# A two-layer attention and retention trunk: tokens' norm-weight products on GpSimd, norms and rotation tables in numbered rounds, and a first rotation read from PSUM

## The chip, the core and the metric

The kernel runs on one core of one Trainium2 chip. The metric is the device time of one execution in microseconds (us). The engines are named as in the profile: PE is TensorE, PEld its weight loads, DVE is VectorE, ACT is ScalarE, POOL is GpSimd, and SP is SyncE, whose queue issues all DMAs of this kernel. Each engine works through its own instructions in order.

## The reference

The input is a sequence of 2048 tokens of width 1024. Two layers follow one another, and then a last RMS norm. One layer, with `h = RMSNorm(x) * gain`:

```python
proj = h @ w_in                       # 1024 x 4096: aq ak av ag rq rk rv rg, 512 columns each
ya = chunked_rel_attention(aq, ak, av, rel_bias)    # 8 heads x 64, own chunk of 64 and 8 before it
yr = chunkwise_retention(rq, rk, rv, cos, sin)      # 4 heads x 128, q and k rotated, state with decay
y  = concat[ya * silu(ag), yr * silu(rg)]
x  = x + y @ w_out                    # 1024 x 1024
```

The rotation takes the two halves of a head's 128 columns, `t1` and `t2`, to `t1*cos - t2*sin` and `t1*sin + t2*cos`. The angles are the positions times 64 fixed frequencies. All is float32, and the kernel gives every large product in float16 parts: a value is split into an upper half (its float16) and a lower half (the float16 of what remains), and three products (upper-upper, upper-lower, lower-upper) are summed.

## The kernel before, in words

**Tiles and stages.** Tokens lie in 16 tiles of 128, four tiles make a block of 512 (`n` = 0 to 3). A layer's columns are worked in four sections (`s` = 0 to 3): a section has two attention heads and one retention head. For each `(l, s, n)` the kernel runs `dense_T` (L608), which makes the four feature-major products q, k, rotated q and rotated k (`j` = 0 to 3; 24 matmuls of 512 columns each, L731), then `dense_V` (L738), which makes the token-major products of four token tiles (`a` = 0 to 3; values and gates, 24 matmuls each, L752). The attention and retention of block `n` run beside the dense products of block `n + 1`. After the four sections of a layer, `wout` multiplies by `w_out`.

**Rounds.** `dense_T` and `dense_V` are generators that yield after every eight matmuls of 512 columns. `run` (L1176) takes one such step, then `tick` (L598), which executes what was put off with `later(k, ...)` for k rounds, then one step of the attention (a unit takes three rounds: scores, maximum, exponential, split, transpose), and then steps of the background work list `bg` (`push`, `pull`). How many steps it pulls follows from the steps left and the rounds left. I call such a turn a round. Round 0 is the first of `dense_V(0, 0, 0)`. Block 1 has rounds 12 to 23 (`dense_T`) and 24 to 35 (`dense_V`), block 2 has 36 to 59, block 3 has 60 to 83, and section 1 begins with round 84. The text numbers rounds for both kernels in this way; the kernel before does not count them.

**The order of the engines** is the program's order for PE, ACT, DVE and POOL. SP's order is the program's only up to the end of `dense_V(0, 0, 0)` (`sp_order`, L1245 and L1446); after that the framework's planner places the DMAs.

**Start.** The first block's work is written out by hand in a list of steps (L1387 to L1390), of which `d` is a step of the first `dense_T`, `t` of the first rotation table, `xsq4` the squares of token tile 4, and so on. The steps for tiles 4 to 7 go on in a list of twelve rounds (L1392) beside `dense_V(0, 0, 0)`; a `u` in it is a step of the second table, a `bt` one of the bias tiles.

**A token tile's norm.** Tile `t` of `x` is loaded, ACT sums its squares (`sq`), DVE and POOL make the reciprocal root (`root`, a power on POOL, L212), DVE multiplies the tile by the root and the norm's gain (`mul`, L254 or L1207), ACT writes the upper half (`hi`), DVE the lower half (`lo`, L276 or L231), and two DMA transposes bring both into `hT` (`dma`, L236 and L237). Tiles 8 to 15 go through `norms_from_input` (L1190), pushed as background work of 21 steps in blocks 1 and 2, each step together with a step of the next rotation table (`tables`, L83).

**Tables.** `tables(n)` loads 512 positions, makes the angles in two halves of 256 columns, reduces them by multiples of 2 pi on DVE, takes two sines on ACT (L121, L122), negates one on DVE (L124), and writes cosine and sine to DRAM with eight DMAs (L129 to L132). `tab_load` (L613) reads them back for a block.

**Rotation.** In `dense_T`, for `j` = 2 and 3, `evacuate` copies the product from PSUM by ACT (L662). `swap` exchanges the halves of its partitions with two DMAs (L666, L667). Three DVE operations turn it (L686 to L688), and an upper and a lower half follow. For the first block, this begins in round 4 for `j` = 2 and ends in round 14 for `j` = 3. `decayed` (L870) multiplies the rotated k by the rotated q of one token tile; its first call stands in the attention, in round 14.

**Preparation of section 1.** `prep_T` (25 steps) and `prep_V` (23 steps) load and split the next section's weights. PE sums the column squares over partitions with a product with ones (`allsum`, L319), three steps after ACT squared them; `lowp` (L314) casts the sums to bfloat16 before. They are pushed at the start of block 3 and of its `dense_V`.

## Time and profile before

| | us |
|---|---|
| median of 3 runs | 2083.68 (2080.86 to 2083.72) |
| the profiled execution, device time | 2085.9 |
| its span, first to last instruction | 2084.1 |
| PE busy | 2005.3 (96%) |
| DVE busy | 1345.9 (65%) |
| ACT busy | 1141.0 (55%) |
| POOL busy | 435.8 (21%) |
| mean granted PE clock | 0.991 of full speed |

The profile is of one execution. Busy times are shares of the span; an engine's busy time does not say what it waited for, so the stretches with waits are looked up in the timelines of the engines. A row of a timeline gives the start, the duration, the engine, the source line, the operation, the written and read tiles, the shape, and in brackets the idle time ahead of it with what ended it.

### The profile page before, as it was taken

How to read it: one execution, taken by the hardware profiler on the slowest of the kernel's cores; microseconds unless marked ns; L12 is line 12 of the kernel's file. 1: busy time of each engine (PE TensorE's matmuls, PEld its weight loads, DVE VectorE, ACT ScalarE, POOL GpSimd, SP SyncE). 2: the span in 40 equal slices, each digit the busy share in tenths (PEclk: the TensorE clock that was granted, in tenths of full speed). 3: DMA queues.
4: the chain of work that ended last, by engine and by line, in shares of the span. 5: the costliest groups of instructions: out<-in, count | busy, mean ns of one | idle time of the engine just before them, and what ended most of it. 6: DMA issues, size and time to landing. Idle time of an engine off the chain costs nothing. (4 is left out here: it accounts for less than half of the span.)

```text
span 2084.1 us, 39559 instructions
## 1 busy us (share of the span) xinstructions
PE 2005.3 (96%) x14014; PEld 1051.2 (50%) x14014; DVE 1345.9 (65%) x4031; ACT 1141.0 (55%) x2522; POOL 435.8 (21%) x509
## 2 busy tenths in 40 slices
PE   6888999999999999999999999999999999999998
PEld 4334454555555555544444555555555555555443
DVE  7677666666666666676654667666666666667643
ACT  7455565556565654565444546554655665446432
POOL 1022221222122222231000222222222222222100
PEclk9999999999999999999999999999999999999999
DMA  8767775557567764699875556655755766557874
GB/s 250 169 121 164 142 158 113 120 102 158 121 147 147 158 158 99 134 221 256 219 187 118 121 102 138 134 120 102 149 125 125 174 153 166 121 117 176 212 199 124
DMA packets 645702, 313.65 MB, mean 150 GB/s; under 512 B 459232, under 2 KB 602080, under 8 KB 645504
## 3 DMA queue, kind: packets, MB, share of 16 engines
q1 hardware_dynamic: 645504, 311.12, 66.3%
q8 instruction: 110, 1.80, 0.4%
q14 instruction: 88, 0.72, 0.1%
HBM read 123.26 MB, written 41.98 MB: 79 GB/s over the span
## 5 line engine op out<-in xcount | busy, mean ns | idle before, releaser
L810 POOL TENSOR_TENSOR pq<-sc,pq 128x640 f16<-128x640 f32 (+4 forms) x256 | 324.7, 1269 | 1165.6 <-issue 625.4
L807 ACT ACTIVATE sc<-sc,mq,cT 128x640 f32<-128x640 f32 (+4 forms) x256 | 218.5, 853 | 552.0 <-DVE mq L806 416.9
L731 PE MATMUL dT<-hTh,whT 128*128 128x512 f16 x1008 | 351.5, 385 | 15.8 <-DMA hTh<-hTl 9.7
L752 PE MATMUL dV<-whV,hTh 128*128 128x512 f16 x1024 | 352.9, 380 | 10.0 <-DVE gt L770 9.9
L752 PE MATMUL dV<-whV,hTl 128*128 128x512 f16 x1024 | 353.0, 380 | 0.0
L752 PE MATMUL dV<-wlV,hTh 128*128 128x512 f16 x1024 | 352.7, 380 | 0.0
L731 PE MATMUL dT<-hTh,wlT 128*128 128x512 f16 x1008 | 346.6, 379 | 0.0
L731 PE MATMUL dT<-hTl,whT 128*128 128x512 f16 x1008 | 346.6, 379 | 0.0
L752 PEld LDWEIGHTS <-hTh 128*128 128x128 f16 x2048 | 196.6, 98 | 223.1 <-DVE gt L770 13.7
L731 PEld LDWEIGHTS <-whT 128*128 128x128 f16 x2016 | 193.2, 98 | 223.8 <-issue 26.9
L804 DVE CUSTOM_DVE_ANT_0 sc<-S,bias 128x640 f32<-128x640 f32 (+4 forms) x256 | 188.6, 737 | 70.5 <-PE S L801 64.5
L809 ACT ACTIVATE pq<-sc 128x640 f16<-128x640 f32 (+4 forms) x256 | 171.5, 670 | 10.5 <-DMA pT<-pq 2.5
L1129 PE MATMUL dO<-whO,yly 128*128 128x512 f16 x448 | 170.3, 380 | 2.2 <-DMA yly<-rly 1.5
L1129 PE MATMUL dO<-whO,yhy 128*128 128x512 f16 x448 | 170.3, 380 | 0.4 <-DMA yhy<-hTh 0.4
L1129 PE MATMUL dO<-wlO,yhy 128*128 128x512 f16 x448 | 170.2, 380 | 0.0
L752 PEld LDWEIGHTS <-hTl 128*128 128x128 f16 x1024 | 99.5, 98 | 104.0 <-issue 1.4
L731 PEld LDWEIGHTS <-wlT 128*128 128x128 f16 x1008 | 97.3, 98 | 101.8 <-issue 1.1
L800 PE MATMUL S<-k,q 128*128 128x128 f16 (+3 forms) x592 | 143.3, 268 | 1.9 <-DVE mq L804 1.8
L1129 PEld LDWEIGHTS <-yhy 128*128 128x128 f16 x896 | 87.5, 98 | 101.9 <-issue 1.1
L820 PE MATMUL o<-v,pT 128*128 128x65 f16 x1120 | 130.4, 194 | 8.1 <-DMA pT<-pq 7.6
L821 PE MATMUL o<-v,pT 128*128 128x64 f16 x1120 | 130.6, 195 | 0.0
L801 PE MATMUL S<-k,q 128*128 128x128 f16 (+3 forms) x592 | 130.4, 268 | 0.0
(361 smaller groups left out, 3412.0 us busy)
## 6 DMA issues: line engine op xcount, KB each, us to landing
q<-qq SPq DMA_DIRECT2D x128, 128.0 KB, 2.6
yyy<-y_d SPq DMA_DIRECT2D x32, 512.0 KB, 4.7
stT<-in_w_in_dram SPq DMA_DIRECT2D x27, 512.0 KB, 4.6
stV<-in_w_in_dram SPq DMA_DIRECT2D x26, 512.0 KB, 4.6
k<-kk SPq DMA_DIRECT2D x128, 64.0 KB, 2.0
swp<-rot SPq DMA_DIRECT2D x64, 128.0 KB, 2.5
tabc<-tab SPq DMA_DIRECT2D x32, 256.0 KB, 2.7
tabs<-tab SPq DMA_DIRECT2D x32, 256.0 KB, 2.9
```

Source lines behind the costliest of these rows:

```text
L731: pe.matmul(ps, w_[:, j, kt, :], h_[:, kt, :], start=(m == 0), stop=(m == 23))
L752: pe.matmul(ps, h_[:, kt, a * P:(a + 1) * P], w_[:, kt, :], start=(m == 0), stop=(m == 23))
L800: pe.matmul(o, st.q[:, hx, 0, cs], k_, start=True, stop=False)
L801: pe.matmul(o, st.q[:, hx, 1, cs], k_, start=False, stop=True)
L804: dve.tensor_tensor_reduce(out=v, in0=S[:, 0:w], in1=g.bias[hx][:, 640 - w:640], scale=1.0, scalar=-3.0e38, op0=ALU.add, op1=ALU.max, accu ...
L807: act.activation(v, v, AF.Exp, bias=m[:, 0:1], scale=g.c[:, 0:1])
L809: act.activation(pq[:, 0:w], v, AF.Copy)
L810: pool.tensor_tensor(pq[:, w:2 * w], v, pq[:, 0:w], op=ALU.subtract)
L820: pe.matmul(o[:, 0:65], u.p[:, b, :], v_[:, 0:65], start=(b == 0), stop=False)
L821: pe.matmul(o[:, 0:64], u.p[:, b, :], v_[:, 65:129], start=False, stop=False)
L1129: pe.matmul(ps, h_[:, kt, :], w_[:, kt, :], start=(m == 0), stop=(m == 23))
```

## The change

What it does, part by part:

- **Products with the norm's gain.** For token tiles 4 to 15 POOL multiplies the tile by the gain, without the root; the root enters as the scale of the ACT copy (upper half) and of the DVE operation (lower half).
- **Numbered rounds.** `run` counts rounds, and `slot(r, fn)` puts work into round r. Tiles 8 to 11 begin their squares in rounds 18, 21, 24, 27, tiles 12 to 15 in rounds 39, 42, 45, 48; each is loaded four rounds earlier, its upper half comes three, its lower half four and its transposes five rounds later. The second table ends in rounds 12 and 14, the third has rounds 18 to 38 and the fourth 36 to 56. The preparation of section 1 is pulled 48 times in rounds 57 to 95. In the list beside `dense_V(0, 0, 0)` the second table's steps rise from ten to fourteen.
- **Cut products.** In block 1, section 0, the products `j` = 0 and 1 are made by token tiles (128 columns), tile 7 last.
- **First rotation.** For the first block, DVE reads the product from PSUM: a cosine product, two half sine products that write to the other half of the partitions, and a sum; there is no copy by ACT and no swap. Both j fall into rounds 3 to 9, the transposes of k into round 11, and the first `decayed` into round 10.
- **Tables.** The negation of a sine is ACT's, directly after the sines, and the cosine is written by one DMA for two copies: six DMAs for eight.
- **Casts of sums.** Where two sums are added and then cast, one DVE operation does both.

The diff, cut to its core:

```diff
@@ tables
         act.activation(r, ang, AF.Sin)
         act.activation(k2, k, AF.Sin)
-        yield
-        dve.tensor_scalar(ang, r, -1.0, None, op0=ALU.mult)
-        yield
+        act.activation(ang, r, AF.Copy, scale=-1.0)
+        yield
+        d = tab_d[n].rearrange("i (b p) (a c) -> i b a p c", b=2, a=2)
         for hf in range(2):
             sl = slice(hf * 64, hf * 64 + 64)
-            cs = slice(hf * 256, hf * 256 + 256)
-            sp.dma_start(tab_d[n][0, 0:64, cs], k2[sl, :])
-            sp.dma_start(tab_d[n][0, 64:128, cs], k2[sl, :])
-            sp.dma_start(tab_d[n][1, 0:64, cs], ang[sl, :])
-            sp.dma_start(tab_d[n][1, 64:128, cs], r[sl, :])
+            sp.dma_start(d[0, :, hf].rearrange("b p c -> p b c"), k2[sl, None, :].to_broadcast([64, 2, 256]))
+            for b, t_ in enumerate((ang, r)):
+                sp.dma_start(d[1, b, hf], t_[sl, :])
@@ Tok
         def mul(self):
+            if self.rows:
+                pool.tensor_tensor(self.x, self.x, gains[0].b, op=ALU.mult)
+                return
...
-                act.activation(self.rw[0], self.x, AF.Copy)
+                rows_hi(self.rw, self.x, self.r)
...
-                dve.tensor_tensor(self.rw[1], self.x, self.rw[0], op=ALU.subtract)
+                rows_lo(self.rw, self.x, self.r)
@@ sums and casts
-        if len(sts) == 2:
-            dve.tensor_tensor(m1[:, 0:1], m1[:, 0:1], m1[:, 1:2], op=ALU.add)
-        return m1[:, 0:1]
+        return [m1[:, i:i + 1] for i in range(len(sts))]
...
+        if more is None:
+            dve.tensor_copy(mb, m1)
+        else:
+            dve.tensor_tensor(mb, m1, more, op=ALU.add)
@@ dense_T
+        def first_rotation(j, ps, rot):
+            if j == 2:
+                st.rq = rot
+                later(1, tab_load)
+                own = rot[:, 1:3].rearrange("p a c -> p (a c)").bitcast(F32)
+            else:
+                st.rk = rot
+                own = b1.tile([P, 512], F32, tag="qq", name=f"raw{nm}")
...
+            def cosine():
+                dve.scalar_tensor_tensor(out=own, in0=ps, scalar=2.0 ** -16, in1=st.tabc, op0=ALU.mult, op1=ALU.mult)
+
+            def sine(half):
...
+                dve.scalar_tensor_tensor(out=st.swp[o_], in0=ps[i_], scalar=-2.0 ** -16, in1=st.tabs[i_], op0=ALU.mult,
+                                         op1=ALU.mult)
...
+            d = 2 * j
+            later(d, cosine)
+            later(d, lambda: sine(0))
+            later(d + 1, lambda: sine(1))
+            later(d + 2, lambda: dve.tensor_tensor(own, own, st.swp, op=ALU.add))
+            later(d + 3, lambda: act.activation(rot[:, 0], own, AF.Copy))
+            later(d + 4, lambda: dve.tensor_tensor(rot[:, 1], own, rot[:, 0], op=ALU.subtract))
+            if j == 2:
+                later(d + 5, lambda: act.activation(rot[:, 2], rot[:, 0], AF.Copy, scale=2.0 ** -11))
+            else:
+                later(d + 6, tokens)
...
+        parts = (l, s, n) == (0, 0, 1)
+        if parts:
+            ps, m = [None] * 2, 0
+            for (j, a) in ((0, 0), (0, 1), (0, 2), (1, 0), (1, 1), (1, 2), (0, 3), (1, 3)):
...
+                    pe.matmul(ps[j][:, cs], w_[:, j, i % KT, :], h_[:, i % KT, cs], start=(i == 0), stop=(i == 23))
+                    m += 1
+                    if m % 32 == 0 and m < 192:
+                        yield
+                if a == 3:
+                    evacuate(j, ps[j])
+            yield
@@ attention
-            elif a == 0 and (l, s, n) == (0, 0, 0):
-                decayed(l, s, n, g, st, 0)
@@ run
+            for fn in slots.pop(ring["round"], ()):
+                fn()
+            ring["round"] += 1
+            if left is None:
+                continue
@@ norms_from_input
+            def mul():
+                pool.tensor_tensor(u.x, u.x, gains[0].b, op=ALU.mult)
+
+            for i, fn in ((-4, load), (0, sq), (0, mul), (1, root), (3, lambda: rows_hi(rows, u.x, u.rs)),
+                          (4, lambda: rows_lo(rows, u.x, u.rs)), (5, lambda: transpose_rows(rows, *u.h))):
+                slot(r + i, fn)
@@ steps and rounds
-       "Vhi2 Vhi3 d d Vlo2 Vlo3 xsq5 d Vu d xsq6 xrs4 d Vu xmul4 xsq7 d")
+       "Vhi2 Vhi3 d d Vlo2 Vlo3 xsq5 xmul4 d Vu d xsq6 xrs4 xmul5 d Vu xsq7 xmul6 d")
-    push(rounds(["xhi4 xrs5 xrs6", "xlo4 xmul5 xrs7", "xdma4 xhi5 xmul6 bt", "xlo5 xhi6 u", "xdma5 xlo6 xmul7", "xdma6 xhi7",
-                 "xlo7", "xdma7 u", "u u bt", "u u bt", "u u", "u u bt"]), 12)
+    push(rounds(["xhi4 xrs5", "xlo4 xrs6 xmul7", "xdma4 xhi5 xrs7 bt", "xlo5 u", "xdma5 xhi6 u", "xlo6 u", "xdma6 xhi7 u",
+                 "xlo7 u u", "xdma7 u u bt", "u u bt", "u u", "u u bt"]), 12)
+    table_steps(t1, (12, 12, 14))
+    table_steps(t2, [18] + list(range(22, 36)) + [36, 38])
+    table_steps(t3, [36] + list(range(40, 54)) + [54, 56])
+    norms_from_input(18, range(8, 12), late[0:4])
+    norms_from_input(39, range(12, 16), xs0[0:2])
+    first_prep = 57
+    for r in range(first_prep, 96):
+        for _ in range((r + 1 - first_prep) * 48 // 39 - (r - first_prep) * 48 // 39):
+            slot(r, lambda: pull(1))
+    slot(first_prep - 1, lambda: push(prep_T(0, 1, grp(0, 1)), 25))
...
-                if (n, s) == (0, 0) and not first:
+                if (n, s) == (0, 0):
                     later(11, lambda n=n, g=g, st=st: decayed(l, s, n, g, st, 0))
```

129 lines of the change are left out of this document (61 added, 68 removed).

## The prediction

> **What bounds the kernel now.** I read the page's first part, then the waits of TensorE, then busy time by windows cut at the points where TensorE changes its token block, then the engines' timelines around each hole. TensorE is the bound:
>
> ```profile
> PE 2005.3 (96%) x14014; PEld 1051.2 (50%) x14014; DVE 1345.9 (65%) x4031; ACT 1141.0 (55%) x2522; POOL 435.8 (21%) x509
> 360.00:2084.10 1724.10, 1699.36 (x11882) 886.82 (x11879) 1098.92 (x3279) 929.38 (x2068) 367.96 (x412) 1.00 0.66 148
> 47.70:78.50 30.80, 21.10 (x97) 9.21 (x96) 18.71 (x38) 14.61 (x31) 1.90 (x5) 0.89 0.84 188
> 78.50:140.40 61.90, 51.95 (x293) 25.18 (x294) 46.35 (x135) 35.22 (x75) 10.88 (x18) 0.94 0.60 129
> 140.40:206.60 66.20, 57.47 (x398) 29.98 (x398) 46.54 (x127) 36.14 (x75) 15.50 (x18) 0.91 0.73 150
> 206.60:260.00 53.40, 48.51 (x352) 25.65 (x353) 33.21 (x113) 31.12 (x68) 11.98 (x11) 0.95 0.71 144
> 260.00:360.00 100.00, 95.41 (x703) 50.65 (x701) 65.10 (x235) 59.98 (x145) 22.39 (x30) 1.00 0.63 136
> ```
>
> In a window's row the first number is its length, the second TensorE's busy time, and the number after POOL's the granted clock. From 360 us on TensorE is idle for 1724.1 - 1699.4 = 24.7 us of 1724, and there the change only swaps tiny casts. Between 47.7 and 360 us the idle time is 9.7 + 9.9 + 8.7 + 4.9 + 4.6 = 37.9 us, at a clock of 0.89 to 0.95 up to 260 us. This is the whole of the first weight section and the preparation of the second, and it is where the change works. What is saved in it moves all later TensorE work earlier, one for one. The two longest entries of TensorE's waits in the same stretch (line waited for: total, times, longest):
>
> ```profile
> PE dT L731 <- DMA hTh<-hTl: 9.7, 1, 9.7
> PE dV L752 <- DVE gt L770: 8.7, 4, 4.9
> ```
>
> The holes and what follows them, from TensorE's timeline (start, duration, count, idle before):
>
> ```profile
> 31.02 0.61 PE L712 MATMUL dT<-hTh,whT 128*128 128x128 f16 x8
> 32.35 0.61 PE L712 MATMUL dT<-hTh,whT 128*128 128x128 f16 x8
> ...
> 63.47 0.39 PE L752 MATMUL dV<-whV,hTh 128*128 128x512 f16 x1
> ...
> 68.45 0.38 PE L752 MATMUL dV<-wlV,hTh 128*128 128x512 f16 x1
> 78.52 3.57 PE L731 MATMUL dT<-hTh,whT 128*128 128x512 f16 x8 [9.69 <-DMA hTh<-hTl]
> ...
> 129.53 0.39 PE L752 MATMUL dV<-whV,hTh 128*128 128x512 f16 x1 [4.88 <-DVE gt L770]
> ...
> 140.36 3.47 PE L731 MATMUL dT<-hTh,whT 128*128 128x512 f16 x8 [2.44 <-issue]
> ...
> 146.31 1.89 PE L731 MATMUL dT<-hTl,whT 128*128 128x512 f16 x8
> ...
> 182.67 0.22 PE L860 MATMUL r<-sh,rot 128*128 128x128 f16 x1 [1.90 <-DVE sh L868]
> 194.32 0.39 PE L752 MATMUL dV<-whV,hTh 128*128 128x512 f16 x1 [2.68 <-DVE gt L770]
> 206.64 3.57 PE L731 MATMUL dT<-hTh,whT 128*128 128x512 f16 x8 [3.65 <-DMA hTh<-rhn]
> ```
>
> Between 63.47 and 68.45 lie 23 starts, 0.217 us each: a tile's 24 matmuls take 5.2 us and a round, a third of them, 1.73. Eight as one row show 1.89 us in a running stream and 3.47 to 3.57 right after a hole: each hole costs 1.6 us more at a lowered clock. The clock in the windows falls where the holes are. I count six such tails (after 78.5, 129.5, 140.4, 182.7, 194.3 and 206.6 us). That is 9.6 us, and with 33.3 us of idle before 260 us the stake is 43 us. By the Trainium skill, "TensorE: Matmul & The Clock Gate", section "HAM oscillation — how this bites in real kernels", only idle gaps over about 3.4 us are to be avoided; the trace differs, since the hole of 2.4 us before 140.36 has its tail too, and the measurement decides. By the page three tails fewer, 4.8 us, would be at stake.
>
> **Entry of the second token block.** Its first matmul, 78.52, waits for the transposes of token tile 7, although tile 4's products could have run. The change cuts the first two sections' products into token tiles (192 matmuls of 128 columns), tile 7 last. Three groups of eight take 32.35 - 31.02 = 1.33 us, and eight times that is 10.6 us, against two times 5.2 us, so the cut itself costs 0.2 us. The wait for tile 7 goes. What is late next? I follow VectorE, which is in order and runs behind:
>
> ```profile
> 55.47 0.29 DVE L766 SCALAR_TENSOR_TENSOR v<-dV,v 128x128 f16<-128x128 f32 x1 [1.53 <-ACT rv L762]
> 55.68 0.34 DVE L768 SCALAR_TENSOR_TENSOR rv<-dV,urvV,rv 128x128 f16<-128x128 f32 x1
> 55.94 0.41 DVE L770 SCALAR_TENSOR_TENSOR gt<-gt,dV 128x256 f32<-128x256 f32 x1
> 57.46 1.22 DVE L276 TENSOR_TENSOR hTh<-hTh,hTh 128x1024 f16<-128x1024 f32 x1
> 59.00 0.69 DVE L670 TENSOR_TENSOR rot<-rot,tabc 128x512 f32<-128x512 f32 x1 [0.32 <-DMA tabc<-tab]
> ...
> 66.63 0.29 DVE L99 CAST xa<-xa 128x256 f32<-128x256 int32 x1 [1.48 <-DMA xa<-in_pos_dram]
> 66.96 0.35 DVE L100 TENSOR_SCALAR xa<-xa,invf_sb 128x256 f32<-128x256 f32 x1
> 68.61 0.29 DVE L96 TENSOR_SCALAR xa<-xa 128x256 f32<-128x256 f32 x1
> ```
>
> In the changed kernel the first rotation is turned out of PSUM: per section cosine, two half sines and a sum, four operations on 512 columns where there were three, and both sections now fall into rounds 3 to 9 of the first value products; before, the second was turned only in rounds 10 to 14. The operations have 512 columns whatever their partitions, so I give each 0.69 us (59.00). The first decayed product stands in round 10, and it needs the second section's lower half, VectorE's last operation of round 9. Between the gate of tile 0 (55.94, ends 56.3) and that, VectorE has ten operations of 0.69 = 6.9 us, three lower halves of tokens at 1.28 = 3.8 us (1.22 at 57.46; with the scale in them I take 180.00's form, below), two sets of evacuations at 1.04 (55.47 to 55.94) = 2.1 us, and steps 2 to 8 of the second table, some ten operations of 0.29 to 0.43, 3.7 us. That is 16.5 us, less some 0.08 us of overlap between neighbours, 2 us: the half is ready near 71 us, and if the second step waits for its positions as at 66.63, near 72.5. TensorE reaches the product after two thirds of tile 3: 63.47 + 3.46 = 66.9 us. It waits 4 to 5.5 us, where before it ran through to 68.8; one tail of 1.6 follows. I take 4.5 us. A further 1 us is put down for the third section's start: in the cut order section 0's bank is freed just one tile (1.3 us) before it is wanted again, and the copy by ScalarE and the difference by VectorE (0.69 by 59.00) fit into that only if neither engine is behind. So in this window 9.7 + 1.6 goes and 4.5 + 1.6 + 0.2 + 1 comes: **4 us gained**. Its ends are 9.5 (VectorE not behind) and 0 (behind by 4 us more). On SP, four swaps and two writes of each table less are cover for the transposes; I give them nothing, since VectorE comes later.
>
> **Second block's value products, third block's entry.** The hole of 4.9 us before 129.53 waits for VectorE's gate, which waits for ScalarE:
>
> ```profile
> 124.35 1.28 ACT L121 ACT_TABLE_LOAD   x1
> 125.65 0.42 ACT L121 ACTIVATE xb<-xb 128x256 f32<-128x256 f32 x1
> 125.97 0.40 ACT L122 ACTIVATE xb<-xb 128x256 f32<-128x256 f32 x1
> 126.54 1.28 ACT L761 ACT_TABLE_LOAD   x1
> ```
>
> Two table loads and the two sines of a rotation table stand in front of the evacuation. In the changed kernel the sines come in round 12 (second table), 36 (third) and 54 (fourth). 12 and 36 open a feature-major product, whose next evacuation is three rounds (5.2 us) off and covers the 1.28 + 0.42 + 0.40 + 0.42 (the negation, new on ScalarE) + 1.28 = 3.8 us. Round 54 is within a value product, but one third into a tile, the bank wanted six rounds later. The hole of 2.4 us before 140.36 is tile 11's transposes, which come one to two rounds (1.7 to 3.5 us) earlier, in round 32 of 36. VectorE loses four products of 1.28 us in this block. Of 9.95 + 1.6 us in this window I leave 3 us (waits on scores and gates, whose causes stay): **8.5 gained**.
>
> **Third block.** Idle 8.73 us and three tails, 13.5 us: the state's half (1.9), gates, and tile 15's transposes (3.6 before 206.64). Two chains make it:
>
> ```profile
> 180.00 1.28 DVE L1207 SCALAR_TENSOR_TENSOR xin<-xin,rsn,gb 128x1024 f32<-128x1024 f32 x1 [2.55 <-POOL rsn L212]
> 188.00 1.38 DVE L827 TENSOR_TENSOR rl<-rl,kaV 128x1 f32<-128x1 f32 x1
> 179.41 0.55 POOL L212 TENSOR_TENSOR rsn<-ssn,mhalf 128x1 f32<-128x1 f32 x1
> 187.97 1.40 POOL L810 TENSOR_TENSOR pq<-sc,pq 128x640 f16<-128x640 f32 x1 [4.54 <-ACT pq L809]
> L810 POOL TENSOR_TENSOR pq<-sc,pq 128x640 f16<-128x640 f32 x192 | 271.7, 1415 | 861.0 <-issue 469.1 <-ACT pq L809 374.0 <-DMA y_d<-ya 11.2
> L1058 POOL TENSOR_TENSOR hTl<-hTl,fg 128x512 f32<-128x512 f32 x1 | 1.3, 1262 | 3.9 <-ACT fj L1054 3.9
> L827 DVE TENSOR_TENSOR rl<-rl,kaV x256: 159/159/1376, 99.0 to 1959.9; 128x1 f32<-128x1 f32 x128
> ```
>
> At 180.00 VectorE stands 2.55 us for GpSimd's root before it can multiply the token; in the changed kernel the product needs no root, is GpSimd's own, and the root enters in ScalarE's copy two rounds later. Tile 15's transposes go out in round 53 of 60 instead of about 58. I leave 5 us of the 13.5, one late start with its tail and a little more: **8.5 gained**. The cost is on GpSimd: 128x1024 by twice L1058 is 2.5 us a token, against 1.28 on VectorE. With 1.4 (L810) and two roots of 0.55 it comes to 4.5 us in a step of three rounds, 5.2 us at least; it is queued right behind the unit's difference, so it fills the gap before the next.
>
> **Preparation of the next section.** 4.9 us of idle plus a tail after 206.6: 48 steps come over 39 rounds instead of 48 over 24, so the three steps between a section's squares and TensorE's sum over them are 2.4 rounds instead of 1.5. Half goes, with the tail: **4 gained**. The casts of sums save one 128x1 operation each on VectorE, nothing on the path. After 260 us: 0.
>
> **Sum.** 4 + 8.5 + 8.5 + 4 = 25 us. The profiled execution took 2085.9 us (2084.1 of span, 1.8 around it), the median of the runs is 2083.7; the gain is the same in both: 2061 profiled, 2059 as a median.
>
> **Rivals.** *GpSimd's products hold VectorE (slower).* At 187.97 GpSimd starts a difference of 1.40 us, and VectorE's one-column product at 188.00 takes 1.38 us instead of its median 0.16. So VectorE stands for as long as GpSimd runs. Twelve products of 2.5 us could hold it 30 us, against 12 x 1.28 = 15 us of work taken off it. If TensorE pays every hold in full, 30 - 25 = 5 us slower, and with a clock tail of 1.6 at half the tokens 10 more: 2083.7 + 15 = 2099. It decides from a cost of 25 / 12 = 2.1 us a token on TensorE's path. Against it: GpSimd's differences, 192 of them of 1.4 us, run through the whole kernel already, and L827's median equals its minimum. By the Trainium skill, "SBUF — State Buffer", section "SBUF: two separate sides", the loser of the pair of ports that VectorE and GpSimd share is blocked for the whole instruction; by that rule every lower half and table step that meets a product waits it out. The trace agrees at 188.00. *The wait only moves (faster, by less).* The first decayed product takes the whole first window and each later block keeps one late start of some 4 us with its tail: 4 + 8.5 + 8.5 + 4 less 4 + 5.6 + 5.6 is 10 us, 2074. For it speaks VectorE's 46 of 62 us in the second block; against it, 5 us of products leaving there. *It doesn't start earlier.* SP, whose order after the first block is not written out, lets transposes stand behind other transfers, and rounds gained are lost there: 0 to 4 us, 2082.
>
> **Numbers.** Forecast 0.72, 2045 to 2071 (all 43 us but 4, to half of the 25); moved wait 0.13 (2071 to 2079); not earlier 0.06; held VectorE 0.09. Less than 0.2%, 4.2 us, can't be told from no change here. Faster 0.86 (forecast, moved wait, a little of the third), same 0.05, slower 0.09. The range 2045 to 2080 leaves out the slower rival, most of the third and a thin tail below.
>
> **What would show it.** Right: section products of the second block start near 72 to 75 us; TensorE waits on VectorE's half in the first decayed product, 4 to 5 us; no ScalarE table load between a value product and its evacuation in the second block; no hole over 2 us before the third and fourth block; the idle from 47.7 to 260 us falls from 33 to near 15. Wrong: VectorE rows stretched to 2 us and more beside GpSimd's products, and TensorE waiting on gates or on the transposed probabilities in rounds 18 to 50; or idle time from 360 us on that differs from 24.7 us by more than 3.

## The result and the profile after

The changed kernel is slower, by a little. Eleven runs have a median of 2089.78 us (2083.75 to 2092.8), eleven of the kernel before on the same chip 2083.68 us; the ratio on record, formed from all these runs, is 1.0022, with a 95% interval of 1.0012 to 1.0031 (the two medians alone are 6.1 us apart). Three later timings of the same program beside the kernel before gave 1.0015 (1.0007 to 1.0024), 1.0018 (1.0006 to 1.0029) and 1.0009 (0.9999 to 1.002). By these ratios the loss is 2 to 5 us, about 3.5, where 25 us of gain were forecast. The profiled execution took 2090.2 us.

The first row is from the page of the changed kernel, the others from its busy time by windows, cut where TensorE enters the second, third and fourth block, section 1's feature-major products, its value products, and at 360 us (columns as in the windows of before):

```profile
PE 2005.6 (96%) x14158; PEld 1056.5 (51%) x14158; DVE 1346.3 (64%) x4004; ACT 1141.7 (55%) x2524; POOL 465.5 (22%) x521
47.80:77.60 29.80, 23.17 (x101) 9.85 (x100) 24.35 (x49) 15.25 (x33) 10.65 (x12) 0.91 0.72 143
77.60:137.30 59.70, 52.04 (x435) 31.52 (x434) 43.05 (x114) 32.61 (x72) 20.70 (x19) 0.93 0.57 124
137.30:203.30 66.00, 55.09 (x402) 28.61 (x400) 46.97 (x119) 38.98 (x80) 26.24 (x21) 0.97 0.81 171
203.30:258.60 55.30, 52.87 (x410) 28.51 (x411) 39.25 (x134) 35.69 (x79) 13.92 (x13) 1.00 0.75 163
258.60:293.60 35.00, 28.25 (x206) 14.57 (x204) 18.40 (x68) 23.01 (x51) 8.47 (x10) 0.95 0.61 136
293.60:360.00 66.40, 65.16 (x451) 34.24 (x451) 43.27 (x160) 35.84 (x88) 12.77 (x18) 0.97 0.55 121
360.00:2088.40 1728.40, 1697.47 (x11871) 885.47 (x11868) 1092.49 (x3260) 927.45 (x2065) 365.89 (x411) 1.00 0.67 148
```

TensorE is idle for 6.6, 7.7, 10.9 and 2.4 us in the first four windows, 27.6 in all, where the kernel before had 33 up to 260 us and the forecast 15. The new hole is in the fifth window: 35.0 us for twelve rounds, with 6.8 idle and a clock of 0.95. The kernel before needs 27.7 there (a window of its own trace):

```profile
267.00:294.70 27.70, 26.36 (x204) 14.06 (x202) 15.42 (x60) 19.41 (x46) 6.99 (x8) 1.00 0.77 168
```

The holes of the changed kernel, from TensorE's timeline:

```profile
65.29 0.39 PE L808 MATMUL dV<-whV,hTh 128*128 128x512 f16 x1 [1.75 <-DVE gt L826]
70.06 0.29 PE L914 MATMUL r<-rot,rot 128*128 128x128 f16 x2 [1.14 <-ACT rot L659]
74.08 0.29 PE L914 MATMUL r<-rot,rot 128*128 128x128 f16 x1 [3.74 <-DVE rot L660]
...
117.19 0.22 PE L914 MATMUL r<-sh,rot 128*128 128x128 f16 x1 [2.24 <-DVE sh L922]
...
127.83 0.61 PE L808 MATMUL dV<-whV,hTh 128*128 128x512 f16 x1 [3.61 <-DVE gt L826]
...
177.07 0.27 PE L856 MATMUL S<-k,q 128*128 128x256 f16 x1 [3.86 <-DVE mq L860]
...
184.61 0.22 PE L914 MATMUL r<-sh,rot 128*128 128x128 f16 x1 [1.31 <-DVE sh L922]
...
193.75 0.39 PE L808 MATMUL dV<-whV,hTh 128*128 128x512 f16 x1 [1.81 <-DVE gt L826]
...
203.26 1.04 PE L787 MATMUL dT<-hTh,whT 128*128 128x512 f16 x4 [2.47 <-DVE gt L826]
...
283.93 0.16 PE L328 MATMUL msV<-mbV,ones 128*128 128x1 bf16 x1 [3.00 <-DVE mbV L318]
...
293.59 2.63 PE L808 MATMUL dV<-whV,hTh 128*128 128x512 f16 x7 [3.70 <-ACT whV L335]
```

The hole of 9.7 us before the second block is gone. In its place stand 1.75, 1.14 and 3.74 us within the first value products; in the second and third block nearly every wait is for VectorE (state's halves, gates, the maximum `mq`); and 3.00 and 3.70 us wait for section 1's value weights.

One profile of each kernel is not enough for differences of some us, so both were profiled again, unaltered. The table gives the start in us of the first matmul of each stretch, for three profiles of before and four of after; the last column is the time from the third section's first matmul to the end of the span.

| | 2nd block | 3rd block | 4th block | section 1 | its values | 3rd section | from there to the end |
|---|---|---|---|---|---|---|---|
| before | 78.5, 78.4, 76.7 | 140.4, 140.6, 139.0 | 206.6, 205.3, 203.5 | 266.9, 264.7, 261.3 | 294.7, 292.5, 289.1 | 476.8, 473.4, 470.0 | 1607.3, 1610.9, 1606.8 |
| after | 77.6, 78.1, 78.2, 78.7 | 137.3, 137.8, 137.7, 138.2 | 203.3, 205.4, 205.4, 205.8 | 258.6, 260.7, 260.6, 261.6 | 293.6, 295.7, 295.7, 296.6 | 475.1, 477.9, 477.1, 479.0 | 1613.4, 1611.5, 1611.1, 1605.3 |
| difference of means | +0.3 | -2.3 | -0.2 | -4.0 | +3.3 | +3.8 | +2.0, within the scatter |

The result is in the middle columns: 4.0 us are gained by section 1's start, 7.2 are lost in its first products (35.0 us in all four profiles, 27.7 to 27.8 in the three of before), and 3.3 remain, about the loss that the timings show.

### The profile page after: what moved, and what is told of

Read it like the earlier page. It is cut to its first block, busy times and chain, and to the rows that moved or that the text cites. A ratio compares the mean times of both kernels' runs of the same rounds, so it can differ in the third digit from the quotient of the medians.

```text
span 2088.4 us, 39808 instructions
## 1 busy us (share of the span) xinstructions
PE 2005.6 (96%) x14158; PEld 1056.5 (51%) x14158; DVE 1346.3 (64%) x4004; ACT 1141.7 (55%) x2524; POOL 465.5 (22%) x521
## 4 chain that ended last, share of the span: by engine, by line
PE 44%; DVE 3%; DMA 3%; ACT 3%; issue 2%; SPq 1%; POOL 0%; POOLq 0%; DVEq 0%; ACTq 0%
PE dT L787 14%; PE dV L808 12%; PE dO L1183 12%; PE r L914 2%; PE S L857 1%; PE S L856 1%; DMA pT<-pq 1%; DMA swp<-rot 1%; PE o L876 1%; PE o L877 1%; PE o L878 1%; ACT sc L863 1%; DVE sc L860 1%; ACT pq L865 0%; DMA x_d<-hTl 0%
## 5 line engine op out<-in xcount | busy, mean ns | idle before, releaser
L787 PE MATMUL dT<-hTh,whT 128*128 128x512 f16 x992 | 342.4, 380 | 2.5 <-DVE gt L826 2.5
L787 PE MATMUL dT<-hTl,whT 128*128 128x512 f16 x992 | 342.4, 380 | 0.0
L787 PE MATMUL dT<-hTh,wlT 128*128 128x512 f16 x992 | 342.2, 379 | 0.0
L860 DVE CUSTOM_DVE_ANT_0 sc<-S,bias 128x640 f32<-128x640 f32 (+4 forms) x256 | 188.3, 735 | 77.9 <-PE S L857 66.1
L856 PE MATMUL S<-k,q 128*128 128x128 f16 (+3 forms) x592 | 142.4, 267 | 5.0 <-DVE mq L860 5.0
L876 PE MATMUL o<-v,pT 128*128 128x65 f16 x1120 | 129.7, 193 | 16.8 <-DMA pT<-pq 16.5
L876 PEld LDWEIGHTS <-pT 128*128 128x128 f16 x1120 | 105.4, 97 | 54.9 <-DMA pT<-pq 26.2
```

The costliest lines, as they stand in the source:

```text
L787: pe.matmul(ps, w_[:, j, kt, :], h_[:, kt, :], start=(m == 0), stop=(m == 23))
L856: pe.matmul(o, st.q[:, hx, 0, cs], k_, start=True, stop=False)
L860: dve.tensor_tensor_reduce(out=v, in0=S[:, 0:w], in1=g.bias[hx][:, 640 - w:640], scale=1.0, scalar=-3.0e38, op0=ALU.add, op1=ALU.max, accu ...
L876: pe.matmul(o[:, 0:65], u.p[:, b, :], v_[:, 0:65], start=(b == 0), stop=False)
```

## The experiments

Each kernel was timed beside the kernel before on the same chip, and each ratio is to that; medians of different rows can come from different chips. In the expectations, "second section" is section 1, and the stretch "from about 476 us" (464 in the faster kernels) begins with the third section.

| kernel | median us | ratio to before (95%) |
|---|---|---|
| changed, again (e1, e15, e16) | 2087.40, 2086.60, 2085.86 | 1.0015, 1.0018, 1.0009 |
| value weights earlier (e2) | 2082.24 | 0.9989 (0.9979 to 0.9999) |
| products on VectorE (e3) | 2090.69 | 1.0026 (1.0016 to 1.0036) |
| both (e4) | 2085.94 | 1.0005 (0.9996 to 1.0014) |
| weights earlier, no products (e5) | 2072.90 | 0.9946 (0.9932 to 0.9960) |
| weights earlier, decayed product later (e6, e10) | 2075.61, 2075.10 | 0.9958 (0.9944 to 0.9972), 0.9959 (0.9943 to 0.9975) |
| changed, decayed product later (e12) | 2080.93 | 0.9991 (0.9982 to 0.9999) |
| as e6, uncut (e17) | 2075.17 | 0.9961 (0.9948 to 0.9975) |
| as e6, sines later (e18) | 2074.63 | 0.9961 (0.9949 to 0.9974) |
| before, again (e13, e14) | 2083.41, 2081.62 | 0.9994 (0.9986 to 1.0003), 0.9992 (0.9982 to 1.0003) |

### The preparation of section 1

```diff
-    for r in range(first_prep, 96):
-        for _ in range((r + 1 - first_prep) * 48 // 39 - (r - first_prep) * 48 // 39):
-            slot(r, lambda: pull(1))
+    for r0, r1, k in ((first_prep, 72, 25), (72, 90, 23)):
+        for r in range(r0, r1):
+            for _ in range((r + 1 - r0) * k // (r1 - r0) - (r - r0) * k // (r1 - r0)):
+                slot(r, lambda: pull(1))
```

> Only the pace of the second section's weight preparation is altered: the 25 steps of the feature weights in rounds 57 to 71, the 23 of the value weights in rounds 72 to 89, where the changed kernel spreads 48 evenly and ends in round 95, the last before the second section's value products. Theory (what the first section saves is given back because the value weights come by rounds): the wait of 3.0 us for the sum over the squares at 283.9 and of 3.7 us for the last converted weights at 293.6 go, the value products start 6 to 7 us sooner, near 287 us, and the time falls by about as much, 2083 to 2084. Rival (the preparation only fills VectorE and ScalarE, which are behind anyway; packing it into fewer rounds makes gates late in the fourth block): the fourth block grows by 3 to 5 us and the total stays within 2 us of the changed kernel.

Measured: section 1's first products take 28.0 us instead of 35.0, and the time is 5.2 us below that of the changed kernel beside it (2082.24 and 2087.40). The theory holds for the two waits. But the first half of the rival holds too: the fourth block takes 59.3 us where the changed kernel has 55.3, since TensorE waits again for the sums over the squares, four times, 1.1 to 1.6 us. Fourth block and first products together fall from 90.3 to 87.3 us, by 3 and not by 7 (from 90.8 in the twelfth run to 86.0 in the sixth and tenth, below). What makes the rest of the 5.2 us is open: the fourth block begins 3.5 us sooner in this profile than in that of the changed kernel beside it, before the packed steps can have saved anything. ScalarE's timeline shows the chain, first in the changed kernel (with VectorE's cast of the sum, and the two GpSimd operations ahead of the bias tile's scaling):

```profile
281.33 0.83 ACT L584 ACTIVATE bias<-bias,ciT 128x640 f32<-128x640 f32 x1 [1.97 <-DMA y_d<-ya]
282.55 1.04 ACT L310 ACTIVATE whV<-stV 128x1024 f16<-128x1024 f32 x1
...
290.69 1.13 ACT L335 ACTIVATE whV<-stV,sV 128x1024 f16<-128x1024 f32 x1
...
292.40 1.14 ACT L335 ACTIVATE whV<-stV,sV 128x1024 f16<-128x1024 f32 x1
...
283.71 0.16 DVE L318 TENSOR_TENSOR mbV<-m1V,m1V 128x1 bf16<-128x1 f32 x1 [5.35 <-ACT whV L310]
...
279.49 1.40 POOL L866 TENSOR_TENSOR pq<-sc,pq 128x640 f16<-128x640 f32 x1 [5.57 <-issue]
...
281.15 0.14 POOL L583 MEMSET bias<- 64x64 f32 x1
```

the same scaling in the second profile of the changed kernel:

```profile
283.41 0.83 ACT L584 ACTIVATE bias<-bias,ciT 128x640 f32<-128x640 f32 x1 [1.97 <-POOL bias L583]
```

and with the earlier preparation:

```profile
268.50 1.04 ACT L310 ACTIVATE whV<-stV 128x1024 f16<-128x1024 f32 x1
...
278.34 1.14 ACT L335 ACTIVATE whV<-stV,sV 128x1024 f16<-128x1024 f32 x1
...
286.01 0.83 ACT L584 ACTIVATE bias<-bias,ciT 128x640 f32<-128x640 f32 x1 [1.97 <-POOL bias L583]
```

In the changed kernel the square of the last value section stands in the program behind the scaling of a bias tile, and that waits until 281.33. The row names a transfer, `y_d<-ya`, but the scaling does not use that tile. What it waits for is GpSimd, which fills two corners of the bias tile behind its difference and ends at 281.29; the second profile names it, with the same 1.97 us. The square then ends at 283.6, TensorE's sum over it comes 3.00 us late, the two conversions at 290.69 and 292.40 follow, and the last of them is what the value products wait for at 293.59. With the steps packed into fewer rounds the square is at 268.5, the conversion at 278.3, and the bias tile comes after both, though its scaling waits the same 1.97 us.

### The products with the norm weights

```diff
-                pool.tensor_tensor(self.x, self.x, gains[0].b, op=ALU.mult)
+                dve.tensor_tensor(self.x, self.x, gains[0].b, op=ALU.mult)
...
-                pool.tensor_tensor(u.x, u.x, gains[0].b, op=ALU.mult)
+                dve.tensor_tensor(u.x, u.x, gains[0].b, op=ALU.mult)
```

In the fifth kernel both lines are left out instead.

> Only the engine of the twelve products of a token with the norm weights is altered: VectorE in place of GpSimd, in the same rounds, still without the root. Theory (GpSimd's products of 2.4 us each hold VectorE's two-operand work, so that they cost it 1.9 us a token beyond its own work, more than the 1.28 us they take off it): the eight stretched rows of VectorE (2.1 to 2.65 us at 95, 103, 114, 124, 161, 170, 182 us, 1.6 at 154) are gone; TensorE's waits of 2.2, 3.6, 3.9 and 1.3 us at 117, 128, 177 and 185 us shrink to half or less, and the second section's first block starts 3 to 6 us sooner, near 254 us. Rival (VectorE is simply full: 1.28 us of product there is as bad as the hold): it starts within 1.5 us of 258.6. By the theory that the second section's value products wait for weights that come by rounds, the time itself stays within 2 us of the changed kernel in either case, since the start of the value products stays bound.

> Both alterations together: value weights finished by round 89 and the products on VectorE. If both theories hold, the second section's first block starts near 254 us and its value products near 282, 11 us before the changed kernel; the time is 2078 to 2081. If only the preparation counts, it is that of the earlier preparation alone, 2083 to 2084. If neither, 2088 to 2091.

> The earlier value weights of the second run, and the twelve products of a token with the norm weights left out altogether (the norm weights then act only through the other factors, so the output is another one). It gives the whole price of the products: on GpSimd by comparison with the earlier preparation alone, on VectorE by comparison with that and the products on VectorE. Theory (the hold is paid on the path: eight rows of VectorE stretched by 1.6 to 2.4 us, TensorE's waits at 117, 128, 177 and 185 us behind them): the second section's first block starts 6 to 9 us sooner than with GpSimd's products, at 252 to 255 us, and the time falls by 4 to 8 us to 2074 to 2078. Rival (VectorE is late in these blocks with or without them, since rotations, tables and gates come in the same rounds): it starts at 259 to 261 us and the time stays within 2 us of 2082.

The hold that all three speak of, from GpSimd's and VectorE's timelines of the changed kernel, with a row of the same form beside each that meets no product:

```profile
113.98 2.40 POOL L1273 TENSOR_TENSOR xin<-xin,gb 128x1024 f32<-128x1024 f32 x1 [1.11 <-ACT hTh L203]
123.48 2.76 POOL L1273 TENSOR_TENSOR xin<-xin,gb 128x1024 f32<-128x1024 f32 x1 [1.11 <-ACT hTh L203]
103.27 2.12 DVE L883 TENSOR_TENSOR rl<-rl,kaV 128x1 f32<-128x1 f32 x1
111.17 0.16 DVE L883 TENSOR_TENSOR rl<-rl,kaV 128x1 f32<-128x1 f32 x1
114.45 2.48 DVE L718 TENSOR_TENSOR rot<-rot 128x512 f16<-128x512 f32 x1
129.41 0.69 DVE L718 TENSOR_TENSOR rot<-raw,rot 128x512 f16<-128x512 f32 x1
124.14 2.65 DVE L712 TENSOR_TENSOR raw<-raw,swp 128x512 f32<-128x512 f32 x1
118.62 0.68 DVE L712 TENSOR_TENSOR raw<-raw,tabc 128x512 f32<-128x512 f32 x1
```

VectorE's lower half at 114.45 takes 2.48 us, where the same operation takes 0.69 at 129.41; it ends 0.55 us behind GpSimd's product (116.38), about its own time. Eight rows of the second and third block are stretched so, at 95, 103, 114, 124, 154, 161, 170 and 182 us, by 15 us together.

Yet the theory of the third run fell: with the products on VectorE the holes are as long, only for other operands. The rival is right in that VectorE's own time for the products is as bad as the hold, but it is worse than it said: section 1 starts at 263.6 us, outside both forecasts (near 254, or within 1.5 of 258.6), and later than the 260.7 of the changed kernel beside it. The time is 3.3 us worse (2090.69 and 2087.40), where both had it within 2 us, and 3.7 us worse with the earlier weights (2085.94 and 2082.24), which is none of the three cases that the fourth run's expectation names. TensorE's timeline of the third run:

```profile
114.81 0.33 PE L914 MATMUL r<-rot,rot 128*128 128x128 f16 x3 [2.87 <-DVE dT L922]
...
130.12 0.61 PE L808 MATMUL dV<-whV,hTh 128*128 128x512 f16 x1 [4.95 <-DVE gt L826]
...
165.46 0.33 PE L914 MATMUL r<-rot,rot 128*128 128x128 f16 x3 [2.41 <-DVE dT L922]
...
181.12 0.37 PE L856 MATMUL S<-k,q 128*128 128x256 f16 x1 [3.53 <-DVE mq L860]
```

Without the products the time falls by 9.3 us to 2072.90, more than the 4 to 8 of the theory; section 1 starts at 255.3 us, and the third section 6.5 us sooner than with GpSimd's products, so some 3 us of the difference belong to the later stretch, where single executions scatter. TensorE's time in the second and third block, all three with the earlier weights, first on GpSimd, then on VectorE, then without, from the windows of each:

```profile
76.84:135.58 58.74, 48.67 (x435) 29.98 (x433) 42.75 (x113) 32.30 (x72) 20.70 (x19) 1.00 0.57 124
135.58:201.87 66.29, 54.99 (x399) 28.68 (x399) 46.76 (x120) 39.30 (x80) 26.26 (x21) 0.97 0.80 172
```

```profile
76.42:137.54 61.12, 50.31 (x435) 30.43 (x433) 39.23 (x117) 32.37 (x72) 10.67 (x15) 0.97 0.54 120
137.54:206.56 69.02, 55.30 (x399) 28.78 (x399) 42.95 (x124) 39.29 (x80) 16.38 (x17) 0.98 0.79 165
```

```profile
80.52:133.76 53.24, 49.13 (x435) 30.78 (x433) 35.46 (x113) 32.23 (x72) 10.11 (x15) 0.98 0.64 137
133.76:195.97 62.21, 54.82 (x399) 28.73 (x399) 39.29 (x120) 39.14 (x80) 16.16 (x17) 0.97 0.85 174
```

Eight products cost TensorE (58.7 - 53.2) + (66.3 - 62.2) = 9.6 us on GpSimd and (61.1 - 53.2) + (69.0 - 62.2) = 14.7 on VectorE, though no wait in the changed kernel's trace ends with GpSimd's product itself. Of a hold of 1.9 us, up to 1.2 show on TensorE, although VectorE is busy for only 43 of 59 and 47 of 66 us. (The second block of the run without products starts 3.7 us later, by a gate; at section 1's start 5.9 of the 9.6 us and 10.8 of the 14.7 are left, so both are upper ends.)

### The first decayed product

```diff
-                if (n, s) == (0, 0):
+                if (n, s) == (0, 0) and not first:
                     later(11, lambda n=n, g=g, st=st: decayed(l, s, n, g, st, 0))
...
             if hx == 1:
                 next(ret, None)
+            elif a == 0 and (l, s, n) == (0, 0, 0):
+                decayed(l, s, n, g, st, 0)
```

> The earlier value weights, and the first decayed product back where the kernel before had it, in the first attention unit's second round instead of round 10 of the first value products. In the changed kernel TensorE waits there 3.7 us at 74.1 for VectorE's lower half, and 1.1 us just before. Theory (that wait is VectorE's lateness at this one place, and a product asked for four rounds later finds its operand ready): both waits go, the second block starts 3.5 to 5 us sooner, at 72 to 73.5 us, and the time falls by 3 to 5 us to 2077 to 2079. Rival (VectorE is late for the next user too, the gates and scores of the second block, so the wait only moves): the second block starts sooner, but its value products start within 1.5 us of 100 us, and the time stays within 1.5 us of 2082.

> The changed kernel with only the first decayed product back in the attention unit, and the preparation as the change has it. Theory (gains in the first section are given back at the second section's value products, whose weights come by rounds): the second block starts near 72 us, 5 us sooner, and the second section's first block near 253 us, but its value products wait longer, and the time falls by no more than 3 us, to 2085 to 2088; with the earlier preparation the same step was worth 6.6 us. Rival (the two gains add): 2081 to 2083.

> The same kernel without the extra transfers, once more beside it: 2074 to 2077, and a second sample of its stretch from about 464 us to the end (1613 us in the first).

The first two run with and without the earlier weights, the third repeats the first. The second block starts at 71.5, 72.3 and 72.6 us, 5 to 7 sooner than in the changed kernel, behind one wait for a gate there (the sixth run's timeline):

```profile
71.50 0.62 PE L767 MATMUL dT<-hTh,whT 128*128 128x128 f16 x8 [1.52 <-DVE gt L826]
```

The time falls by 6.6 us with the earlier weights, where 3 to 5 were expected, and without them to a ratio of 0.9991, where the changed kernel has 1.0009 to 1.0022: by 4 to 6.5 us. So the theory of the twelfth run was wrong: the loss at the value products does not swallow what is gained ahead of it. Its products took 35.0 us again, starting from 254.2. The preparation is tied to rounds, rounds move with TensorE, and the 7.2 us are a fixed price; the gains add. The change with these two edits, the sixth and tenth run, is 0.4% faster than the kernel before.

### The cut and the sines

```diff
-        parts = (l, s, n) == (0, 0, 1)
+        parts = False
```

> Earlier value weights and the first decayed product in the attention unit, and the second block's first two sections uncut again, as in the kernel before: 24 matmuls of 512 columns each, the lower halves of the tokens last in the first section. With the cut the second block starts at 71.5 to 72.6 us, and token tile 7's two transposes land about 1.2 us before and 1.5 us after that. Theory (the earlier norms and the shorter queue on SP did away with the hole of 9.7 us, the cut does nothing here): the second block starts within 1 us of 72, the third block within 1 us of where it does with the cut (131.2 to 132.9), the time is 2074 to 2077. Rival (the cut is needed): a hole of 2 us or more at the start, and the third block starts 2 us or more later, 2077 to 2080.

The second block starts at 72.6 us and the third at 132.8, as in the tenth run with the cut (72.6 and 132.9), and the time is the same. The cut does nothing in this kernel. The issue of tile 7's last transpose ends at 72.2 us here (70.96 + 1.24) and at 77.3 in the kernel before (74.34 + 2.93), so the hole of 9.7 us went because the transposes come earlier. The changed kernel as it was, with the decayed product in round 10, was not run without the cut.

```diff
-    table_steps(t3, [36] + list(range(40, 54)) + [54, 56])
+    table_steps(t3, [36] + list(range(40, 54)) + [56, 57])
```

> The same two edits with the cut, and the third table's sines in round 56 and its writes in round 57, where the change has rounds 54 and 56. In round 54 two loads of ScalarE's function table of 1.28 us and three operations of 0.4 stand ahead of the evacuation of the third block's third tile, and TensorE waits 2.47 us at the start of the fourth block for the bank. Theory (the loads make that hole): it falls under 0.5 us, the fourth block starts 2 to 2.5 us sooner, 195 to 197.5 us, and the time falls by 2 us to 2072 to 2074. Rival (ScalarE or VectorE is late there anyway): the hole stays over 1.5 us and the time within 1 us of 2075.

The changed kernel's ScalarE, ahead of its hole of 2.47 us at 203.26:

```profile
197.29 1.28 ACT L121 ACT_TABLE_LOAD   x1
...
200.26 1.28 ACT L817 ACT_TABLE_LOAD   x1
201.56 0.47 ACT L817 ACTIVATE gt<-dV,ughV 128x256 f32<-128x256 f32 x1
201.93 0.36 ACT L818 ACTIVATE rv<-dV,urvV 128x128 f16<-128x128 f32 x1
```

(The expectation counts the tables from 0; it is the fourth.) With the sines in round 56 the hole is gone and the fourth block starts at 195.6 us, 1.8 and 3.6 sooner than in the sixth and the tenth run. But a sum for the weights waits 2.17 us a little later:

```profile
200.73 0.16 PE L328 MATMUL msT<-mbT,ones 128*128 128x1 bf16 x1 [2.17 <-DVE mbT L316]
```

Section 1 starts at 255.7 us (256.8 and 258.6), and the time of 2074.63 can't be told from 2075.1. The theory holds for the hole; the 2 us that it put on the time are not shown.

### The stretch after 475 us

> The changed kernel once more, unaltered. It separates what is in the program from what differs between executions. If the loss after 475 us is part of the program (instructions arriving 6 us earlier or later fall differently against the probability transposes), the second profile again starts the second section's first block near 258.6 us and its value products near 293.6, and again spends 4 to 6 us more than the kernel before between 475 us and the end. If it is scatter between executions, the landmarks up to 475 us agree within 0.5 us and the stretch from there to the end differs from the first profile by several us. Time by either: 2084 to 2092.

> The earlier value weights, and twelve loads' worth of extra transfers of 512 bytes each, one in each round from the third on of the second section's second block (about 322 to 345 us): as many as the change took off SP's queue. All waits on probability transposes after 475 us that the five changed kernels show and the kernel before does not (at about 491, 525, 908, 950, 1296, 1711, 1912 us) come from instructions that are the same in both. Theory (it is SP's place in its own instruction stream: its fetches of 16 KB every 17 us each hold it for about 1 us, and fall on other transfers when there are fewer instructions ahead of them): twelve more shift them back, most of these waits go, and the time falls to 2077 to 2080. Rival (the loss comes with the buffers' other places, or with the moment at which the stretch begins): the waits stay where they are, and the time is 2082 to 2083.

> The kernel before with four extra transfers of 512 bytes in the same place, rounds 3 to 6 of the second section's second block; nothing before 320 us differs. It gives the semaphores of all later transfers the places that they have in the changed kernel (eight in turn, and twelve fewer is four on), and shifts SP's instruction stream by four transfers. Theory (the later loss is a matter of SP's place in its stream or in the turn of semaphores): waits on probability transposes appear at about 491, 525, 908 and 950 us, and the time rises by 3 to 6 us to 2087 to 2090. Rival (it comes with other buffers or another starting moment): the tail is as in the kernel before, 2083 to 2085.

> Earlier value weights, first decayed product in the attention unit, and twelve extra transfers of 4 bytes kept in their places in SP's order, between about 275 and 340 us (in the run with twelve transfers they had gone ahead of the second block, and cost 17 us there). Theory (the later loss is a matter of SP's place in its instruction stream or of the turn of semaphores, which twelve transfers fewer had shifted): from the second section's last block (about 464 us) to the end it takes some 1606 to 1608 us, as the kernel before does, where the same kernel without them takes 1610 to 1613; the time falls to 2071 to 2073. Rival (the later loss has another cause): 1610 to 1613 and 2075 to 2077.

> The kernel before with four extra transfers of 4 bytes kept in their places at about 322 to 335 us; nothing ahead of them differs. Theory (turn of semaphores or place in the instruction stream): the stretch from about 476 us to the end grows from 1607 to 1610 to 1613 us, and the time to 2087 to 2090. Rival: unchanged within 1.5 us, 2083 to 2086.

> The kernel before against itself. If the later loss is scatter between executions, its stretch from about 476 us to the end is anywhere between 1606 and 1613 us, like that of the changed kernels. If it belongs to the program, it is 1606 to 1609 us again. The ratio of times should hold 1 within 0.001.

> As the copy before it: a third profile of the kernel before, 1606 to 1609 us from about 476 us to the end if the difference belongs to the program, up to 1613 if it is scatter.

> The changed kernel unaltered, third profile. If the later loss belongs to the program: 1611 to 1614 us from about 476 us to the end. If scatter: as low as 1607 in one of this and the next. The second section's first product block again takes 35 us, where the kernel before takes 28.

> The changed kernel unaltered, fourth profile, to be read with the third: 1611 to 1614 us for the stretch from about 476 us to the end if the later loss belongs to the program, as low as 1607 if it is scatter between executions.

The edit of the runs with extra transfers (the `tc.keep_in_program_order` and the single element are those of the later two):

```diff
                 if (l, s, n) == (0, 1, 1):
+                    dum = dp.tile([16, 1], F32, tag="dum", name="dum")
+                    for i in range(12):
+                        later(3 + i, lambda i=i: tc.keep_in_program_order(sp.dma_start(dum[i:i + 1, :], invf_sb[0:1, :])))
```

The first profiles suggested that the program loses some 6 us after 475 us, in places where it is the same as before: over the whole span TensorE waited 16.5 us for transposed probabilities instead of 7.6. The theory that SP's place in its instruction stream does it fell. The first pair of these runs says little, since the planner moved the transfers to 25 to 41 us, ahead of the second block (it starts at 95.6 us with twelve of them, and the time is 2096.31 us; 2089.39 with four in the kernel before). In the second pair, where they stayed in place, twelve changed nothing (2076.32 and 2075.10 without), and four in the kernel before made 2086.25 us, 1.0013 (1.0001 to 1.0025), no clear change; from the third section to the end these two took 1607.0 and 1610.3 us. What those numbers are worth is shown by the plain copies: the changed kernel's stretch took 1613.4, 1611.5, 1611.1 and 1605.3 us, that of before 1607.3, 1610.9 and 1606.8, and the sixth and tenth run, one program, 1613.2 and 1607.0. It is scatter of 6 to 8 us between executions of one program. A mean difference of 2 us could hide in it and stays open.

## Why the prediction was wrong, step by step

As means of the profiles, the terms 4 + 8.5 + 8.5 + 4 + 0 became -0.3 + 2.5 - 2.1 + 3.8 - 7.2 = -3.3 us. The entry, the cost of GpSimd's products in the two blocks, and the time after 260 us went wrong; the last of them turned the sign.

**Entry of the second block: 4 us gained, measured none (78.1 against 77.9 us).** The hole of 9.7 us went, as said, but the cut is not needed for it. The wait on VectorE's half in the first decayed product came, with 3.74 us and 1.14 for ScalarE's copy ahead of it, 4.9 in all where 4 to 5.5 were forecast. What the sum left out is the gate before it, 1.75 us at 65.29. And the hole that went was 8.9 and 7.6 us long in the two other profiles of before, not 9.7. The term was mis-sized by 4 us; it came out at its lower end, 0.

**Second and third block: 8.5 and 8.5 us gained, measured 2.5 and -2.1.** The step that failed is the cost of GpSimd's products, "it fills the gap before the next": that reckoned with GpSimd's own queue and put the cost on VectorE at nothing. (Its own sum for GpSimd, 2.5 + 1.4 and two roots of 0.55, makes 5.0 us and not 4.5, in a step of 5.2.) Its price is up to 9.6 us of TensorE's time for eight products. On VectorE the same products cost up to 14.7, so taking them to GpSimd is worth some 5 us. The products are not the whole of what is missing from the 17: without any, the two blocks take 53.2 and 62.2 us, 8.9 and 2.9 less than the means of before. The fourth table's sines, below, are a part of the other 5 us; the rest, in waits for gates and `mq`, was not taken apart. The rival that names the mechanism (VectorE held for as long as GpSimd runs) had a chance of 0.09 and a hold of 30 us for twelve products; eight are in these blocks, held for 15 us, and at most two thirds of that reached TensorE: 1.2 us a token, below its point of 2.1. It did not make the kernel slower by itself. The prediction had the row that should have weighed more, 187.97 and 188.00, and set it aside because GpSimd's differences run through the whole kernel already. By the Trainium skill, "SBUF — State Buffer", section "SBUF: two separate sides", whichever of the two takes the shared pair of ports first keeps it for its whole instruction; the rows at 114.45 and 124.14 agree.

**The fourth table's sines: covered, measured 2.5 us.** The prediction held that in round 54 "the bank wanted six rounds later" covers two table loads. The bank of the tile under way was wanted by the next block's first section, and ScalarE's gate stood behind the loads. For the second table (round 12) and the third (round 36) the step was right: no table load stands between a value product and its evacuation there.

**Preparation, fourth block: 4 us gained, measured 3.8** (55.4 against 59.2 us as means). This step was right, but it is one trade with the next: with the steps packed into fewer rounds the fourth block takes 59.3 us again.

**After 260 us: 0. Measured 7.2 us lost.** This is the step that turned the sign. The working followed the 48 steps up to the start of section 1 and took their slower pace as a gain only. It did not ask when the last of them is wanted: the first value products come in round 96, the last steps in round 95, and from the last square to the end of the last conversion ScalarE's chain takes 11 us (282.55 to 293.54), six rounds; with the earlier steps it takes as long (268.50 to 279.48), but is out of the way. In the kernel before the last conversion ends just as the value products begin (294.74), without a wait, from ScalarE's timeline:

```profile
293.46 1.13 ACT L330 ACTIVATE whV<-stV,sV 128x1024 f16<-128x1024 f32 x1
```

"After 260 us: 0" was written without a row.

**The base.** The forecast counted holes of one profile of before, in which section 1 begins at 266.9 us. Two more give 264.7 and 261.3, so some 2.6 us of the 43 at stake were scatter.

**Signs.** Of the five, the wait in the decayed product came; section products from 72 to 75 us (77.6), no hole over 2 us before the third and fourth block (2.47 before the fourth, and in the three further profiles also 2.4 before the third, behind VectorE's `ya`) and idle time near 15 us (27.6) did not come; the one on table loads in the second block held. Both signs of a wrong forecast came: VectorE's rows of 2 us and more, and idle time after 360 us of 30.9 instead of 24.7. The latter is scatter: it is 24.9 to 30.9 us in the four profiles and 24.7 to 27.3 in the three of before.

**The clock.** The prediction counted a tail of lowered clock after each hole from 1.9 us up. In the changed kernel eight matmuls after the hole of 2.47 us take 1.90 us, full speed, and after that of 3.00 us the starts are 0.43 us apart:

```profile
284.33 0.63 PE L787 MATMUL dT<-hTh,whT 128*128 128x512 f16 x1
284.76 0.63 PE L787 MATMUL dT<-hTh,wlT 128*128 128x512 f16 x1
```

By the Trainium skill, "TensorE: Matmul & The Clock Gate", section "HAM oscillation — how this bites in real kernels", idle gaps of over about 3.4 us are the ones to avoid. The hole of 2.47 us agrees; the one of 3.00 us here, and that of 2.44 before 140.36 in the kernel before, do not.

Not tried apart: the casts of sums, the six instead of eight writes of a table, and the first rotation from PSUM.

## What to carry to other kernels

Work spread evenly up to its deadline has no slack left: when steps are moved to numbered rounds, count back from the first user of the last result through every engine in between, and look at what stands ahead of it in the same queue. Packing the steps has a price as well: it saved 7 us at the deadline here and cost 4 where they were packed. An operation moved from VectorE to GpSimd was not off VectorE's path here; such a move is best priced by a run without it beside one run on each engine. And take two or three profiles of the kernel before, before single holes of 2 us are added up.

## What the hardware showed that was not expected

The same program, at the same granted clock (1.00 in this stretch), took 1605.3 to 1613.4 us for one stretch of identical instructions. Why is open. One thing that differs is SP: one transfer's issue takes 1.81 us in one execution and 0.33 in another. From SP's timeline, first of the changed kernel, then of its third profile:

```profile
406.67 1.81 SPq L619 DMA_DIRECT2D tabc<-tab  x1
```

```profile
408.68 0.33 SPq L619 DMA_DIRECT2D tabc<-tab  x1
```

It does not explain the scatter: the third profile's stretch took 1611.1 us, and the fourth, with 1.81 us again, has the shortest, 1605.3. Nor is the cause of the longer issue shown. The page of transfers has one fetch of instructions (16 KB; 111 of them in the span) close to this transfer in the first profile, and one in the third as well.
